# SBUF placement of the FFN weights, tile-by-tile pool waits, and a store that changes its engine, in a one-core transformer block

## The chip, the cores and the metric

The program runs on one core of a Trainium2 chip. The metric is device time in microseconds (us) from one launch, as the median of several runs. A profiled execution gives the trace that is read here. The engines are TensorE (PE in the profile; its weight loads are PEld), VectorE (DVE), ScalarE (ACT), GpSimd (POOL) and SyncE (SP), which only issues DMA transfers.

## The reference

The kernel computes one transformer block in float32: 512 tokens, a width of 2048, and a hidden width of 5632.

```python
mod_x = jnp.split(silu(c) @ w_ada + b_ada, 6, -1)          # and the same for the context
px = modulate(x, sh1, sc1) @ w_in                          # 2048 -> 7168; context: 4096 columns
ox = bidirectional gated linear attention, 8 heads, states from the 256 context tokens
yx = concat([ox, pool mixer, short convolution]) @ w_out   # 2048 -> 2048
x  = layer_norm(ALPHA * x + g1 * yx)
u, g = split(modulate(x, sh2, sc2) @ w_up)                 # 2048 -> 2 x 5632
fx = (u * silu(dwconv3(g) + b)) @ w_down                   # convolution along rows of 64 tokens
return layer_norm(ALPHA * x + g2 * fx)
```

About half of the time goes into the last two products, `w_up` and `w_down`.

## The kernel before

Every large product is made of three float32r matmuls (`mm3`, L109 to L113): both operands are split into a rounded high part and the rest, and hi x hi (L111), hi x lo (L112) and lo x hi (L113) are added in PSUM. In a matmul one operand is stationary (128 x 128, loaded ahead) and the other moves through (256 or 512 columns).

The stages, with the times of the profiled execution:

- 0 to 396 us, ramp: the first modulations and products with `w_in` (tiles `rc`, `rx`, `px_*`).
- To 900 us, attention heads (`lv`, `Q`, `T`, `U`) mixed with further products; then the local mixers.
- About 1000 to 1360 us: `out_half` (`w_out`), `norm_mid` (layer norm, modulation, transposes; writes the activations `h2h`, `h2l`), and `up_half` for the first four of 44 row blocks of `w_up`, which covers the time until all activations exist. `combine` makes the sums S1 to S4 of activations.
- 1375 to 2191 us, up blocks: `up_pair` (L1029) for 20 pairs of row blocks, each with one `up_block` (L997) for the gate half (`ub_g`) and one for the value half (`ub_u`). An up block multiplies 2 x 2 blocks with seven products in place of eight. Its weights are the stationary operand. `weights7` (L976 to L995) loads a tile W (two DMAs, 1 MB together, from SP, L986), combines it on DVE (L989 to L991), and `parts` splits it into H (ACT cast, L972) and L (DVE subtraction, L973). There are 2 buffers of W and 3 each of H and L; one W gives two H and two L. Each up block takes 168 matmuls of 256 columns: 72 with `h2` as the moving operand, 96 with S1 to S4.
- DVE and ACT then put the gate together (L935 to L937, L1038, L1039) and DVE multiplies u with it (L1044); the result h is stored to DRAM (L1045, 256 KB each).
- 2191 to 2644 us, `down` (L1101): h comes back from DRAM (`hr`, L1064) and is split into `hh`, `hl` (or `hb`, both halves in one tile from another pool, for some row blocks). Here h is the stationary operand, and the weights of `w_down` (tiles H_dn, L_dn) move with 512 columns. The work is cut into portions of 15, 14, 12 and 3 row blocks; the last is `finish` (L1122) with the closing layer norm.

Tiles come from pools. Some stacks of pools grow from the left end of SBUF, others from the right. When a pool ends, the next one gets its memory; before that the wait was one for all: the first tile of the new pool waits until every operation on the old pool is done. The scheduler sets the order of each engine's instructions from the program and priorities; `high_priority(offset=AHEAD)` puts the loads and splits of weights ahead of their place. SP's queue runs in order: an issue that waits holds up all behind it.

Addresses: each partition's tiles start at multiples of 32 bytes, and nearly all tiles are multiples of 512 bytes long, so a few small tiles at the start of a stack (`edge_right`, `edge_left`, columns of constants) set the start of everything above, modulo 512. Before, the right side starts at 384 (activations `a2`, S1 to S4, `hh`, `hl`, all weights) and the `h2` and `hb` tiles on the left at 448.

Of the kernel before, what the change touches and what calls it, by code (L numbers as in the profile page):

```python
# [9 lines left out]
F32 = mybir.dt.float32  # L10
# [6 lines left out]
P = 128  # L17
# [26 lines left out]
def vw(ap, dims, off=0):  # L44

    return bass.AP(tensor=ap.tensor, offset=ap.offset + off,
                   ap=[list(ap.ap[0])] + [list(d) for d in dims])
# [25 lines left out]
class Kernel:  # L73
    def __init__(self, ctx, tc, I, out):
        self.tc, self.nc, self.I, self.out = tc, tc.nc, I, out
        self.ctx = ctx
        self.persist = ctx.enter_context(tc.tile_pool(name="persist", bufs=1))
        self.edge = ctx.enter_context(tc.tile_pool(name="edge", bufs=1, side="right"))
        self.edge.tile([P, 24], F32, name="edge_right")
        self.acts = ctx.enter_context(tc.tile_pool(name="acts", bufs=1, side="right"))  # L80
        self.dram = ctx.enter_context(tc.tile_pool(name="spill", bufs=1, space=bass.MemoryType.DRAM))
        self.ps = ctx.enter_context(tc.tile_pool(name="ps", bufs=1, space=PSUM))
        self.ahead = 0
# [51 lines left out]
    def setup(self):  # L135
        nc, I, pp = self.nc, self.I, self.persist
        self.ident = pp.tile([P, P], F32, name="ident")
        make_identity(nc, self.ident)
        self.ones = pp.tile([P, 32], F32, name="ones")
        nc.vector.memset(self.ones, 1.0)  # L140
        self.ones_r = pp.tile([P, P], F32R, name="ones_r")
        nc.scalar.copy(out=self.ones_r, in_=vw(self.ones[:, :], [[0, 4], [1, 32]]))
        self.mhalf = pp.tile([P, 4], F32, name="mhalf")
        nc.vector.memset(self.mhalf, -0.5)
        self.zero = pp.tile([P, 1], F32, name="zero")
        nc.vector.memset(self.zero, 0.0)
        self.cols = {}
        self.persist.tile([P, 8], F32, name="edge_left")

    def columns(self, pool, parts, name):  # L150

# [788 lines left out]
    def up_half(self, cp, p, hf):  # L940

        nc, w = self.nc, self.I["w_up"][0]
        banks = self.banks4(f"up_{p}_{hf}")
        n = 256
        for s in (1, 0):
            for q in (0, 2, 1, 3):
                wh, wl = self.wload(f"up_{p}_{hf}_{s}_{q}",
                                    w[512 * q:512 * q + 512, s * DFF + 256 * p:s * DFF + 256 * p + 256], 4, 256)
                for j in range(4):
                    k = 4 * q + j  # L950
                    h, l = self.h2[hf][k // 2]
                    es = slice((k % 2) * 256, (k % 2) * 256 + 256)
                    for i in range(2):
                        self.mm3(banks[2 * s + i][:, 0:n], (wh[:, j, i * P:(i + 1) * P], wl[:, j, i * P:(i + 1) * P]),
                                 (h[:, es], l[:, es]), start=(k == 0), stop=(k == KT - 1))
        for i in range(2):
            f = 2 * p + i
            u, g = banks[i][:, 0:n], banks[2 + i][:, 0:n]
            c = cp.tile([P, n], F32, name=f"cv_{f}_{hf}", tag="cv", bufs=2)
            s = cp.tile([P, n], F32, name=f"cs_{f}_{hf}", tag="cs", bufs=2)  # L960
            self.gate_conv(f, g, c)
            nc.scalar.activation(out=s, in_=c, func=AF.Sigmoid)
            nc.gpsimd.tensor_tensor(out=s, in0=c, in1=s, op=ALU.mult)
            nc.vector.tensor_tensor(out=c, in0=u, in1=s, op=ALU.mult)
            nc.sync.dma_start(out=self.h_d[f][:, hf * 256:hf * 256 + 256], in_=c)

    def parts(self, ww, name, src, n):

# [60 lines left out]
    def up_pair(self, ww, ep, hx, p):  # L1029
        nc, w = self.nc, self.I["w_up"][0]  # L1030
        g = self.up_block(ww, ep, f"g{p}", w[:, DFF + 256 * p:DFF + 256 * p + 256])
        cs = []
        for i in range(2):
            f = 2 * p + i
            c = hx.tile([P, 512], F32, name=f"cv_{f}", tag="hq", bufs=8)
            s = hx.tile([P, 512], F32, name=f"cs_{f}", tag="hq", bufs=8)
            self.gate_conv(f, g[i], c)
            nc.scalar.activation(out=s, in_=c, func=AF.Sigmoid)  # L1038
            nc.vector.tensor_tensor(out=c, in0=c, in1=s, op=ALU.mult)  # L1039
            cs.append(c)  # L1040
        u = self.up_block(ww, ep, f"u{p}", w[:, 256 * p:256 * p + 256])
        for i in range(2):
            f = 2 * p + i
            nc.vector.tensor_tensor(out=cs[i], in0=u[i], in1=cs[i], op=ALU.mult)  # L1044
            nc.sync.dma_start(out=self.h_d[f], in_=cs[i])  # L1045

    def down_load(self, dn):

# [126 lines left out]
    def run(self):  # L1175
        tc, nc = self.tc, self.nc
        self.setup()
        self.mods2 = self.persist.tile([P, 4 * KT], F32, name="mods2")
        self.o = [None] * KT
        self.h_d = [self.dram.tile([P, L], F32, name=f"h_d{f}") for f in range(NFF)]  # L1180
        self.y_d = [self.dram.tile([P, 4, 512], F32, name=f"y_d{t}") for t in range(NTT)]
        self.g2_d = self.dram.tile([1, D], F32, name="g2_d")
        self.y, self.h2, self.S, self.h = {}, ({}, {}), {}, {}
        self.upc = 0
        with tc.tile_pool(name="wts", bufs=1, side="right") as self.wts:
            with tc.tile_pool(name="xp", bufs=1) as xp:
                self.xp = xp
                with tc.tile_pool(name="rp", bufs=1) as rp:
                    self.setup_columns1(rp)
                    self.load_in(xp, rp)  # L1190
                    self.setup_columns2(rp)
                    T0, V0 = self.ramp(xp, rp)
                with tc.tile_pool(name="gp", bufs=1) as gp:
                    self.bg, self.bg_due, self.tails = self.ada_rest(gp), 0.0, []
                    self.heads(xp, gp, T0, V0)
                    self.local(gp)
                    for _ in self.bg:
                        pass
                    self.split_o()
            hctx = ExitStack()  # L1200
            hx = hctx.enter_context(tc.tile_pool(name="hx", bufs=1))
            with tc.tile_pool(name="cp", bufs=1) as cp:
                st0 = self.out_half(cp, 0)
                self.norm_mid(cp, hx, 0, st0)
                st1 = self.out_half(cp, 1)
                for p in range(SPLIT_PAIRS):
                    self.up_half(cp, p, 0)
                raw = self.norm_mid(cp, hx, 1, st1)
                nc.sync.dma_start(out=self.g2_d.rearrange("o (k p) -> (o p) k", p=P), in_=self.mods2[:, 3 * KT:4 * KT])
                for p in range(SPLIT_PAIRS):  # L1210
                    self.up_half(cp, p, 1)
                    self.combine(cp, raw, (2 * p, 2 * p + 1))
        with tc.tile_pool(name="ww", bufs=1, side="right") as ww:
            with tc.tile_pool(name="ep", bufs=1) as ep:
                for p in range(SPLIT_PAIRS, NFF // 2):
                    self.up_pair(ww, ep, hx, p)
            hctx.close()
            with tc.tile_pool(name="dn", bufs=1) as dn:
                f0 = 0
                for i, n in enumerate(PORTIONS[:-1]):  # L1220
                    self.down(ww, dn, f0, n, i == 0)
                    f0 += n
                self.finish(ww, dn, f0, PORTIONS[-1])
# [28 lines left out]
```

## Time and profile before

| what | value |
|---|---|
| runs | 2696.9, 2699.03, 2702.64 us (median 2699.03) |
| profiled execution | 2703.39 us, its span 2701.6 us, mean granted clock 0.989 |
| PE busy | 2573.6 us, 95% |
| DVE busy | 1895.1 us, 70% |
| ACT, POOL busy | 941.6 us (35%), 225.7 us (8%) |
| HBM read, written | 393.59 MB, 19.93 MB |
| first up block to first down matmul | 1375.0 to 2191.2 us |

How it is read: a window of the trace gives the busy time of each engine in a stretch and, in brackets, the number of instructions. The groups of instructions give the mean duration of one; PE's ends are modelled, and matmuls overlap, so a matmul of 283 ns can start every 119 ns. The chain of waits is followed back from the last instruction and shows at each step what released the next; a wait's row reads total, times, longest. In the names, `ub_g<-h2h,H_g` is: output, moving operand, stationary operand or the reverse.

### The profile page before, as it was taken

What the parts mean: (1) busy time and instruction counts of PE and PEld (TensorE: products, weight loads), DVE (VectorE), ACT (ScalarE), POOL (GpSimd) and SP (SyncE); (2) the same over time, 40 slices, a digit from 0 to 9 for tenths busy, and PEclk for the clock granted to TensorE, in tenths of its full rate; (3) what the DMA queues carried; (4) which work ended last, traced back from release to release, by engine and by line L of the source; (5) the groups of instructions that cost most, each with busy time, mean ns of one, the idle gap of its engine ahead of it and who ended that gap; (6) DMA issues with size and microseconds to landing.
All of it is one profiled execution on the core that took longest, in us unless ns stands there. A gap on an engine that the chain in (4) does not pass through costs nothing.

```text
span 2701.6 us, 40017 instructions
## 1 busy us (share of the span) xinstructions
PE 2573.6 (95%) x16332; PEld 2261.4 (84%) x16332; DVE 1895.1 (70%) x2390; ACT 941.6 (35%) x1127; POOL 225.7 (8%) x207
## 2 busy tenths in 40 slices
PE   5999999999999999989979999999999999999996
PEld 4677978878787787868879999999999988888885
DVE  5534689696968735688888888888888864434338
ACT  4222443232323224444644443443443433222111
POOL 0111022040404000000100000000000000000004
PEclk9999999999999999999989999999999999999998
DMA  8755356646463534666633333333333374333321
GB/s 265 250 194 187 121 198 199 218 136 214 138 221 131 169 97 160 204 213 212 189 104 125 126 103 124 122 106 119 109 122 114 117 245 161 136 121 119 118 94 63
DMA packets 311125, 416.15 MB, mean 154 GB/s; under 512 B 17860, under 2 KB 200476, under 8 KB 310428
## 3 DMA queue, kind: packets, MB, share of 16 engines
q1 hardware_dynamic: 310940, 413.59, 46.6%
q8 instruction: 128, 2.10, 0.3%
q14 instruction: 57, 0.47, 0.0%
HBM read 393.59 MB, written 19.93 MB: 153 GB/s over the span
## 4 chain that ended last, share of the span: by engine, by line
PE 69%; DVE 14%; DMA 8%; issue 5%; ACT 2%; POOL 1%; SPq 1%; DVEq 0%; ACTq 0%; POOLq 0%
PE dn L113 5%; PE dn L112 5%; PE dn L111 5%; PE ub_g L111 3%; PE ub_g L113 3%; PE ub_g L112 3%; DMA W_u<-in_w_up_dram 3%; PE ub_u L111 3%; PE ub_u L113 3%; PE ub_u L112 3%; DMA W_g<-in_w_up_dram 2%; DVE L_g L973 2%; PE wo L112 2%; PE wo L111 2%; PE wo L113 2%
## 5 line engine op out<-in xcount | busy, mean ns | idle before, releaser
L973 DVE TENSOR_TENSOR L_dn<-W_dn,H_dn 128x1536 fp32r<-128x1536 f32 (+1 forms) x56 | 96.2, 1718 | 207.9 <-ACT H_dn L972 207.9
L972 ACT CAST H_u<-W_u 128x1792 fp32r<-128x1792 f32 x80 | 134.1, 1692 | 230.2 <-DVE W_u L991 158.2
L688 DVE SCALAR_TENSOR_TENSOR aacc<-a,csil,aacc 128x512 f32<-128x512 f32 x240 | 180.2, 751 | 12.9 <-DMA a<-in_w_ada_dram 7.5
L973 DVE TENSOR_TENSOR L_u<-W_u,H_u 128x1792 fp32r<-128x1792 f32 x80 | 161.6, 2020 | 38.0 <-ACT H_u L972 38.0
L111 PE MATMUL dn<-H_dn,hh 128*128 128x512 f32 x480 | 186.4, 389 | 1.4 <-ACT hh L1070 1.4
L112 PE MATMUL dn<-L_dn,hh 128*128 128x512 f32 x480 | 187.0, 390 | 0.0
L113 PE MATMUL dn<-H_dn,hl 128*128 128x512 f32 x480 | 186.7, 390 | 0.0
L972 ACT CAST H_g<-W_g 128x1792 fp32r<-128x1792 f32 x80 | 135.2, 1695 | 123.4 <-DVE W_g L991 46.0
L972 ACT CAST H_dn<-W_dn 128x1536 fp32r<-128x1536 f32 (+1 forms) x56 | 81.3, 1451 | 276.2 <-PE dn L113 275.3
L973 DVE TENSOR_TENSOR L_g<-W_g,H_g 128x1792 fp32r<-128x1792 f32 x80 | 161.4, 2018 | 2.4 <-ACT H_g L972 2.4
L111 PE MATMUL ub_g<-h2h,H_g 128*128 128x256 f32 x480 | 135.6, 283 | 14.9 <-ACT H_g L972 14.9
L125 POOL TENSOR_TENSOR ln_r<-ln_e,mhalf 128x1 f32<-128x1 f32 x12 | 9.3, 784 | 1636.0 <-DVE ln_e L120 1405.6
L113 PE MATMUL ub_g<-h2h,L_g 128*128 128x256 f32 x480 | 135.5, 283 | 4.5 <-DVE L_g L973 4.5
L113 PE MATMUL ub_u<-h2h,L_u 128*128 128x256 f32 x480 | 134.3, 280 | 4.4 <-DVE L_u L973 4.4
L112 PE MATMUL ub_g<-h2l,H_g 128*128 128x256 f32 x480 | 134.9, 281 | 0.0
L111 PE MATMUL ub_u<-h2h,H_u 128*128 128x256 f32 x480 | 134.6, 280 | 0.0
L112 PE MATMUL ub_u<-h2l,H_u 128*128 128x256 f32 x480 | 133.9, 279 | 0.0
L106 DVE TENSOR_TENSOR wl_wo<-wr_wo,wh_wo 128x1024 fp32r<-128x1024 f32 x64 | 78.3, 1223 | 49.4 <-ACT wh_wo L105 49.3
L111 PEld LDWEIGHTS dn<-H_dn,hh 128*128 128x128 f32 x480 | 90.1, 188 | 20.6 <-ACT hh L1070 1.8
L113 PEld LDWEIGHTS dn<-H_dn,hl 128*128 128x128 f32 x480 | 90.1, 188 | 19.3 <-DVE hl L1071 0.6
L112 PE MATMUL wo<-wl_wo,oh 128*128 128x512 f32 x256 | 102.7, 401 | 3.7 <-DVE wl_wo L106 3.6
L112 PEld LDWEIGHTS dn<-L_dn,hh 128*128 128x128 f32 x480 | 90.1, 188 | 19.2 <-DVE L_dn L973 0.4
(445 smaller groups left out, 8370.7 us busy)
## 6 DMA issues: line engine op xcount, KB each, us to landing
a<-in_w_ada_dram SPq DMA_DIRECT2D x256, 256.0 KB, 4.3
W_g<-in_w_up_dram SPq DMA_DIRECT2D x80, 512.0 KB, 4.6
W_u<-in_w_up_dram SPq DMA_DIRECT2D x80, 512.0 KB, 4.6
W_dn<-in_w_down_dram SPq DMA_DIRECT2D x24, 1536.0 KB, 6.8
wr_wo<-in_w_out_dram SPq DMA_DIRECT2D x64, 512.0 KB, 4.4
ada<-in_w_ada_dram SPq DMA_DIRECT2D x56, 512.0 KB, 5.0
wr_r<-in_w_in_dram SPq DMA_DIRECT2D x48, 512.0 KB, 3.7
wr_up<-in_w_up_dram SPq DMA_DIRECT2D x32, 512.0 KB, 4.5
```

The lines of the kernel that those rows point to most:

```text
L106: (lo_engine or nc.vector).tensor_tensor(out=lo, in0=raw, in1=hi.bitcast(F32), op=ALU.subtract)
L111: mm(out=out, lhsT=st[0], rhs=mv[0], start=start, stop=False)
L112: mm(out=out, lhsT=st[0], rhs=mv[1], start=False, stop=False)
L113: mm(out=out, lhsT=st[1], rhs=mv[0], start=False, stop=stop)
L125: nc.gpsimd.tensor_tensor(out=r, in0=t, in1=self.mhalf[:, 0:n], op=ALU.pow)
L688: nc.vector.scalar_tensor_tensor(out=acc, in0=raw, scalar=self.csil[:, k:k + 1], in1=acc, op0=ALU.mult, op1=ALU.add)
L972: nc.scalar.copy(out=H[:, 0:n], in_=src)
L973: nc.vector.tensor_tensor(out=Lw[:, 0:n], in0=src, in1=H[:, 0:n].bitcast(F32), op=ALU.subtract)
```

## The change

Three things are done at once.

1. Placement. `edge_right` shrinks from 24 to 16 floats, `edge_left` goes, and a pool `gap` with one tile of 112 floats (448 bytes) is laid on the right side ahead of the pool `ww` (the weights of the up blocks and of the down projection). The activations on both sides now start at 416 modulo 512, the weights in `ww` at 480, the weights of the stages before at 416 or, for the context's first products, at other places.
2. Waits at pool borders. The nine pools outside the persistent ones, and `gap`, get `reuse_waits="tile"`: a new tile waits only for the operations on those old tiles whose memory it takes.
3. The stores of h (L965, L1045; 8 halves and 40 whole tiles) are issued by GpSimd in place of SP.

```diff
-        self.edge.tile([P, 24], F32, name="edge_right")
+        self.edge.tile([P, 16], F32, name="edge_right")
...
-        self.persist.tile([P, 8], F32, name="edge_left")
...
-            nc.sync.dma_start(out=self.h_d[f][:, hf * 256:hf * 256 + 256], in_=c)
+            nc.gpsimd.dma_start(out=self.h_d[f][:, hf * 256:hf * 256 + 256], in_=c)
...
-            nc.sync.dma_start(out=self.h_d[f], in_=cs[i])
+            nc.gpsimd.dma_start(out=self.h_d[f], in_=cs[i])
...
-        with tc.tile_pool(name="wts", bufs=1, side="right") as self.wts:
-            with tc.tile_pool(name="xp", bufs=1) as xp:
+        with tc.tile_pool(name="wts", bufs=1, reuse_waits="tile", side="right") as self.wts:
+            with tc.tile_pool(name="xp", bufs=1, reuse_waits="tile") as xp:
...
+        gap = self.ctx.enter_context(tc.tile_pool(name="gap", bufs=1, side="right", reuse_waits="tile"))
+        gap.tile([P, 112], F32, name="gap_right")
+        with tc.tile_pool(name="ww", bufs=1, reuse_waits="tile", side="right") as ww:
+            with tc.tile_pool(name="ep", bufs=1, reuse_waits="tile") as ep:
...
-            with tc.tile_pool(name="dn", bufs=1) as dn:
+            with tc.tile_pool(name="dn", bufs=1, reuse_waits="tile") as dn:
```

The pools `rp`, `gp`, `hx` and `cp` get the same argument. On PE, DVE and ACT the order of the instructions hardly moves; on SP and POOL the stores do. Line numbers after the change are one lower behind the removed `edge_left`.

SP's queue at the border between `up_half` and the up blocks, before (`wr_up`: weights of up_half, `h_d`: the stored h, `hr`: h for the down projection, `W_g`, `W_u`: weights of the up blocks; in brackets the semaphores that the row waits for):

```order
L100 DMA wr_up_1_0_1_11885<-in_w_up_dram 128x4x256 [waits DMAHW2_49,DVE_49]
L100 DMA wr_up_1_0_3_11915<-in_w_up_dram 128x4x256 [waits DMAHW5_49,DVE_49]
L965 DMA h_d_87<-cv_1_11945 128x256 [waits DVE_49]
L965 DMA h_d_88<-cv_1_11954 128x256 [waits DVE_49]
L1064 DMA hr_20664<-h_d_85 128x512 [waits DMAHW3_49,PE_49]
L986 DMA W_g_0_12023<-in_w_up_dram 128x4x256 [waits DMAHW2_49,DMAHW1_49,DMAHW4_49,DMAHW0_49,DMAHW6_49,DVE_49,DMAHW7_49,PE_49,Pool_49]
L986 DMA W_g_0_12023<-in_w_up_dram 128x4x256
L986 DMA W_g_1_12121<-in_w_up_dram 128x4x256 x2
```

The same place after the change:

```order
L100 DMA wr_up_1_0_1_11884<-in_w_up_dram 128x4x256 [waits DMAHW6_49,DVE_49]
L100 DMA wr_up_1_0_3_11914<-in_w_up_dram 128x4x256 [waits DMAHW7_49,DVE_49]
L1063 DMA hr_20667<-h_d_84 128x512 [waits DMASW4_49,DMASW0_49,PE_49]
L985 DMA W_g_0_12026<-in_w_up_dram 128x4x256 [waits PE_49,Pool_49]
L985 DMA W_g_0_12026<-in_w_up_dram 128x4x256
L985 DMA W_g_1_12124<-in_w_up_dram 128x4x256 [waits DVE_49]
L985 DMA W_g_1_12124<-in_w_up_dram 128x4x256
```

The two stores of h are gone from here, the first W_g waits for PE and POOL alone, and the second one for DVE (the operation S4l, the last of `combine`). On DVE the first operation on W_g stands behind S4l, before and after:

```order
L917 TENSOR_TENSOR S2l_12003<-m_1_7_11382,S2h_12002 128x512 [waits Activation_49]
L917 TENSOR_TENSOR S4l_12007<-a_3_11987,S4h_12006 128x512 [waits Activation_49]
L988 TENSOR_TENSOR W_g_0_12026<-W_g_0_12026 128x4x2x128 [waits DMAHW5_49,DMAHW4_49]
L989 TENSOR_TENSOR W_g_0_12026<-W_g_0_12026 128x4x128 [waits DVE_49]
L990 TENSOR_TENSOR W_g_0_12026<-W_g_0_12026 128x4x128 [waits DVE_49]
```

Only the waits of the row L988 differ from before (it waited for two further transfers and DVE). GpSimd's queue in up_half and the up blocks after the change (`cs`: the gate times its sigmoid, `cv`: the product to be stored):

```order
L962 TENSOR_TENSOR cs_1_11945<-cv_1_11944,cs_1_11945 128x256 [waits Activation_49]
L962 TENSOR_TENSOR cs_1_11954<-cv_1_11953,cs_1_11954 128x256 [waits Activation_49]
L964 DMA h_d_86<-cv_1_11944 128x256 [waits DVE_49]
L964 DMA h_d_87<-cv_1_11953 128x256 [waits DVE_49]
L1044 DMA h_d_88<-cv_12229 128x512 [waits DMASW0_49,DVE_49]
L1044 DMA h_d_89<-cv_12236 128x512 [waits DMASW1_49,DVE_49]
```

The stores follow each other there with nothing between them until the end of the down projection; before, GpSimd had no instruction in the up blocks.

More of the change, by code (lines that the diff above doesn't have):

```diff
@@ L1184, in run @@
         self.upc = 0
-        with tc.tile_pool(name="wts", bufs=1, side="right") as self.wts:
-            with tc.tile_pool(name="xp", bufs=1) as xp:
+        with tc.tile_pool(name="wts", bufs=1, reuse_waits="tile", side="right") as self.wts:
+            with tc.tile_pool(name="xp", bufs=1, reuse_waits="tile") as xp:
                 self.xp = xp
-                with tc.tile_pool(name="rp", bufs=1) as rp:
+                with tc.tile_pool(name="rp", bufs=1, reuse_waits="tile") as rp:
                     self.setup_columns1(rp)
@@ L1192, in run @@
                     T0, V0 = self.ramp(xp, rp)
-                with tc.tile_pool(name="gp", bufs=1) as gp:
+                with tc.tile_pool(name="gp", bufs=1, reuse_waits="tile") as gp:
                     self.bg, self.bg_due, self.tails = self.ada_rest(gp), 0.0, []
@@ L1200, in run @@
             hctx = ExitStack()
-            hx = hctx.enter_context(tc.tile_pool(name="hx", bufs=1))
-            with tc.tile_pool(name="cp", bufs=1) as cp:
+            hx = hctx.enter_context(tc.tile_pool(name="hx", bufs=1, reuse_waits="tile"))
+            with tc.tile_pool(name="cp", bufs=1, reuse_waits="tile") as cp:
                 st0 = self.out_half(cp, 0)
@@ L1212, in run @@
                     self.combine(cp, raw, (2 * p, 2 * p + 1))
-        with tc.tile_pool(name="ww", bufs=1, side="right") as ww:
-            with tc.tile_pool(name="ep", bufs=1) as ep:
+        gap = self.ctx.enter_context(tc.tile_pool(name="gap", bufs=1, side="right", reuse_waits="tile"))
+        gap.tile([P, 112], F32, name="gap_right")
+        with tc.tile_pool(name="ww", bufs=1, reuse_waits="tile", side="right") as ww:
+            with tc.tile_pool(name="ep", bufs=1, reuse_waits="tile") as ep:
                 for p in range(SPLIT_PAIRS, NFF // 2):
```

## The prediction

> **What bounds the kernel now.** I read the page first: the busy shares and the slices.
>
> ```profile
> PE 2573.6 (95%) x16332; PEld 2261.4 (84%) x16332; DVE 1895.1 (70%) x2390; ACT 941.6 (35%) x1127; POOL 225.7 (8%) x207
> PE   5999999999999999989979999999999999999996
> DVE  5534689696968735688888888888888864434338
> ```
>
> TensorE (PE) is nearly always busy, but the average hides two stages with different limits. The windows by stage come next. The first two lie in the up blocks, the third in the down projection.
>
> ```profile
> 1400.00:1700.00 300.00, 300.00 (x2519) 300.00 (x2518) 264.94 (x269) 128.06 (x107) 0.00 (x0) 1.00 0.35 116
> 1700.00:2000.00 300.00, 292.83 (x2443) 291.45 (x2443) 256.70 (x262) 118.48 (x100) 0.00 (x0) 1.00 0.35 115
> 2250.00:2550.00 300.00, 300.00 (x1312) 245.96 (x1311) 117.38 (x124) 66.83 (x59) 0.00 (x0) 1.00 0.37 126
> ```
>
> The columns are PE, weight loads, VectorE (DVE), ScalarE (ACT), GpSimd (POOL), clock, DMA share and GB/s. In the down projection PE is full and nothing else is: a shorter matmul there is a shorter kernel. In the first up window PE is full too, and 300 us over 2519 matmuls are 119.1 ns each, so a pair of blocks (336 matmuls) takes 40.0 us of PE. In the second window PE has gaps. The chain of waits says why; these are the ends of one lap of it:
>
> ```profile
> 1658.40 2.03 DVE L_g L973
> 1660.86 5.57 DMA W_u<-in_w_up_dram
> 1666.53 1.23 DVE W_u L989
> 1671.94 4.56 DMA W_u<-in_w_up_dram
> 1699.04 2.03 DVE L_g L973
> ```
>
> The last subtraction out of a weight buffer (L973) lets the next load into it start, that load lands, DVE combines it, and so on round. From the first to the last row, the same instruction one pair later, are 40.64 us: the feed loop runs a little slower than PE's 40.0 us. The waits in the window 1400 to 2180 agree: PE is kept waiting only by L973, and DVE by the loads.
>
> ```profile
> DVE W_u L989 <- DMA W_u<-in_w_up_dram: 32.3, 38, 2.9
> DVE W_g L989 <- DMA W_g<-in_w_up_dram: 22.5, 23, 2.8
> PE ub_g L113 <- DVE L_g L973: 4.5, 4, 1.7
> PE ub_u L113 <- DVE L_u L973: 4.4, 3, 1.7
> ```
>
> So the up blocks are bound by the feed, with PE close behind. They begin and end at these two starts (chain, then timeline):
>
> ```profile
> 1375.00 0.58 PE ub_g L111
> 2191.18 0.40 PE L111 MATMUL dn<-H_dn,hh 128*128 128x512 f32 x1
> ```
>
> That is 816.2 us for 6720 matmuls, or 121.5 ns of room for each. This is the point from which a slower block matmul costs time; a faster one than 119 brings next to nothing.
>
> **Change, part 1: the pools wait tile by tile.** The one large PE gap that a pool border makes stands ahead of the first up block:
>
> ```profile
> L111 PE MATMUL ub_g<-h2h,H_g 128*128 128x256 f32 x480 | 135.6, 283 | 14.9 <-ACT H_g L972 14.9
> 1363.77 0.61 DVE S4l L918
> 1364.51 0.38 SPq L986
> 1364.95 5.00 DMA W_g<-in_w_up_dram
> 1370.07 1.24 DVE W_g L989
> 1373.26 1.69 ACT H_g L972
> ```
>
> The first weight load is issued only when the last operation of the pools below it (S4l) is done. After the change it waits for an old transpose of norm_mid and for a POOL power; what stands ahead of it in SP's queue is the last load of up_half and a load of h whose stores were out before.
>
> ```profile
> 1337.91 0.81 SPq L965 DMA_DIRECT2D h_d<-cv  x2
> 1339.97 8.59 SPq L100 DMA_DIRECT2D wr_up<-in_w_up_dram  x4
> ```
>
> So it can be issued near 1348.6 and has landed by some 1355. In DVE's order its L989 still follows S4l, so it starts at 1364.4 in place of 1370.07: **5.6 us** earlier. The second weight tile still waits for S4l, and lands 1364.95 + 5.00 = 1369.95 at the latest; DVE needs it only after its three operations on the first. The bounds are 0 (second tile or casts hold it) and 14.9 us (the whole gap). I take 5.6, and since the feed loop begins there, all that follows shifts with it.
>
> At the earlier border (ramp to heads) the chain has a stretch with nothing but issue, and PE waits behind it:
>
> ```profile
> 395.91 1.48 issue
> 397.39 0.68 DVE g L532
> 399.90 1.27 PE lv L573 x7
> PE lv L573 <- DVE Q L589: 4.6, 4, 3.6
> ```
>
> DVE's own work follows it in any case, so of the 3.6 us at most 1.48 can go, and none if another tile's wait ends there: I take **1.0**. At the last border (up to down) PE idles 1.4 us:
>
> ```profile
> L111 PE MATMUL dn<-H_dn,hh 128*128 128x512 f32 x480 | 186.4, 389 | 1.4 <-ACT hh L1070 1.4
> ```
>
> I take **1.0** of it, between 0 and 1.4.
>
> **Part 2: h stored by GpSimd.** Forty stores leave SP's queue in the blocks. SP's wait for them is long but nothing late stands behind it:
>
> ```profile
> SPq L1045 <- DVE cv L1044: 133.5, 38, 7.6
> 1957.86 1.54 SPq L1045 DMA_DIRECT2D h_d<-cv  x2
> 1961.00 0.93 SPq L986 DMA_DIRECT2D W_u<-in_w_up_dram  x2
> DMA to landing us min/median/max: 2.0/2.0/9.1
> ```
>
> The two stores are issued by 1959.40, and the next weight load waits until 1961.00 for its buffer, not for them: gain 0. GpSimd is idle in the blocks (0.00 in the windows), so nothing queues behind the waiting stores there. The stores land 2.0 us after issue, at about 1961.4, just as the weight load starts. If GpSimd's path adds 1 us, they overlap a load of 4.6 us that the loop waits for. Price between 0 and 1 us a pair; I take **0**, as the store is a quarter of the load's size and most of it is out before. The Trainium skill (SBUF — State Buffer, the box on "DVE blocks DMA") speaks against this edit: descriptors of a GpSimd DMA cannot be written while DVE holds the shared port in a two-port mode. DVE does 265 of 300 us here, though in two-operand forms; no run here shows such a store, and by that rule the price is at the upper end, 1 us a pair or above.
>
> **Part 3: placement.** Worked out from pads and tile sizes: in the blocks the stationary weights lay level with the activations S (modulo 512 bytes) and 64 bytes below h2; now 64 above both. In the down projection the weights are the moving operand: the stationary hh, hl lay level with them and hb 64 above; now all lie 64 below. In up_half the 64 below becomes level. What the trace shows of these distances, by form:
>
> ```profile
> L111 PE MATMUL ub_u<-h2h,H_u 128*128 128x256 f32 x478 | 134.0, 280 | 0.0
> L111 PE MATMUL ub_u<-S4h,H_u 128*128 128x256 f32 x160 | 45.4, 284 | 0.0
> L112 PE MATMUL ub_u<-S3l,H_u 128*128 128x256 f32 x160 | 45.3, 283 | 0.0
> L112 PE MATMUL dn<-L_dn,hh 128*128 128x512 f32 x467 | 181.9, 390 | 0.0
> L112 PE MATMUL dn<-L_dn,hb 128*128 128x512 f32 x176 | 69.6, 396 | 0.0
> L111 PE MATMUL rc<-hch,wh_r 128*128 128x256 f32 x240 | 68.5, 285 | 0.0
> L113 PE MATMUL up<-h2h,wl_up 128*128 128x256 f32 x256 | 72.9, 285 | 5.1 <-DVE wl_up L106 5.0
> ```
>
> With the stationary 64 below, a matmul takes 280 against 283.5 level, 3 less; with it 64 above (hb), 396 against 390, 6 more; 128 apart (rc) is like level. Two distances that the change brings in are not shown: 64 above at 256 columns, 64 below at 512.
>
> *Down projection*: 1440 matmuls go from level to 64 below, 528 from 64 above to 64 below. At the price of 256 columns that is 1440 x 3 ns = 4.3 and 528 x (6 + 3) ns = 4.8, together **9.1 us** off. The 144 of the last portion would give 1.3 more, but the chain there runs on DVE, so 0. If instead distance counts without sign, 1440 get 6 ns longer: 8.6 us on. I take the sign as shown and keep both.
>
> *Up blocks*: if the role counts as in hb, 6 ns more on level: 120 + 6 = 126 ns, over the room of 121.5. If it stays in the band of the other distances (280 to 285), the feed hides it. I take **0**: at 256 columns the row that I can see for "apart" is below or at level, and hb differs from hh in its pool and tile shape too. But this is the weakest step.
>
> *up_half*: 768 matmuls 3 ns longer are 2.3 us; DVE makes PE wait 5.0 us there, so part hides: **+1.5**. The projections rc move from 128 to other distances: +-3, taken as 0.
>
> On placement the Trainium skill (TensorE: Matmul & The Clock Gate, Part 2, loading the weights) says that PE reads stationary and moving operand through two independent ports, so that loading one takes nothing from the other. By that the whole of part 3 would be 0; hb against hh, 396 to 390 ns, disagrees.
>
> **Sum** against the profiled execution's 2703.4: -5.6 - 1.0 - 1.0 + 0 - 9.1 + 0 + 1.5 = -15.2 us. That execution lies 4.4 us above the median of the runs, 2699.0, so the median becomes **2684**.
>
> **The rivals.**
>
> *B, block matmuls slow down (slower).* The 64 above at 256 columns costs as in hb: 126.3 ns, 6720 x 126.3 = 848.7 us. PE then sets the blocks' end. Its first 5 us run at half the granted clock, 21 matmuls in place of 42, which is 2.5 us more:
>
> ```profile
> 1375.00:1380.00 5.00, 5.00 (x21) 4.72 (x22) 4.96 (x4) 1.53 (x1) 0.00 (x0) 0.50 0.00 0
> ```
>
> It starts at 1375.0 - 5.6 = 1369.4 and ends at 2220.6, 29.4 later than 2191.2. With -9.1, -2.0 and +1.5 that is +20: **2719**. For it: the only row with this distance. Against it: other columns, other pool. It decides from 121.5 ns on.
>
> *C, placement has no effect* (the two ports of the skill's rule). Left are -5.6 - 1.0 - 1.0: **2691**. Against it stand 280 beside 284 and 390 beside 396.
>
> *D, GpSimd's stores collide with the loads.* The chain lies on the feed loop from about 1650 to 2191, 13 pairs: 13 x 1 us on the forecast, **2697**. Against it: the stores have landed when the load starts, so that only what GpSimd's path adds can overlap.
>
> *E, 512 columns dislike 64 in either direction*: +8.6 in place of -9.1: **2702**. For it: 64 above does cost; against it: h2.
>
> **How the numbers follow.** Forecast 0.40, B 0.24, C 0.14, D 0.10, E 0.12. What the runs can tell from no change is 0.2%, 5.4 us. Faster by more: forecast, C and a little of D, 0.56. Within: most of D and half of E, 0.16. Slower: B and the rest of E, 0.28. The forecast's own range is 2676 to 2691 (first load 0 to 14.9, the down term to 6). To hold eight in ten it must reach up almost to B, and down for a larger gap or down term: 2666 to 2717.
>
> **What would show it.** First step: the idle time ahead of the first ub_g falls from 14.9 to about 9, and the W_g load is issued ahead of S4l. Down term: the dn groups read 386 to 387, with no group at 396. Blocks: the time from the first ub_g to the first dn stays within 2 us of 816; PE waits for L973 remain. If these waits vanish while the windows of the blocks show fewer than 2460 matmuls in 300 us, B holds. If L989 waits longer for its loads than 55 us in all, D holds. What would make the forecast wrong above all is a block matmul over 121.5 ns.

## The result and the profile after

The changed kernel takes 2713.8 us (median of 6, 2710.5 to 2720.7) against 2700.6 us for the kernel before, measured again beside it: a ratio of 1.0052, 95% interval 1.0037 to 1.0067. It is half a per cent **slower**; the forecast was 0.6% faster.

The page of the changed kernel first. PE is busy for nearly as long as before (2560.7 us against 2573.6), DVE too; a software queue for GpSimd's stores is new. The chain of waits is of no use here ("issue 51%"): it loses its thread. That is not the stores' doing, as the kernels e1 and e4 below, with all stores on SP, read 52% and 51%.

```profile
span 2715.1 us, 40075 instructions
PE 2560.7 (94%) x16332; PEld 2239.3 (82%) x16332; DVE 1893.2 (70%) x2390; ACT 938.2 (35%) x1127; POOL 251.9 (9%) x255
q0 software_dynamic: 3584, 11.54, 1.1%
issue 51%; PE 36%; DVE 6%; POOL 3%; ACT 2%; DMA 2%; SPq 0%; POOLq 0%; DVEq 0%; ACTq 0%
L111 PE MATMUL ub_g<-h2h,H_g 128*128 128x256 f32 x480 | 134.3, 280 | 8.8 <-ACT H_g L971 8.8
L111 PE MATMUL ub_u<-h2h,H_u 128*128 128x256 f32 x480 | 132.9, 277 | 0.0
```

The up blocks have moved at both ends (timeline of PE, first block matmul and first matmul of the down projection):

```profile
1361.33 0.58 PE L111 MATMUL ub_g<-h2h,H_g 128*128 128x256 f32 x1 [8.77 <-ACT H_g L971]
2206.04 0.39 PE L111 MATMUL dn<-H_dn,hh 128*128 128x512 f32 x1
```

They begin 13.7 us earlier (1375.0 before) and end 14.9 us later (2191.2): 844.7 us in place of 816.2. From there to the end are 509.1 us, 510.4 before. So the whole loss, and more, lies in the blocks. The windows by stage say what PE does there:

```profile
1365.00:1700.00 335.00, 315.96 (x2674) 312.08 (x2675) 278.62 (x281) 131.79 (x111) 7.63 (x14) 0.98 0.34 111
1700.00:2000.00 300.00, 280.19 (x2364) 276.06 (x2363) 250.17 (x254) 117.04 (x100) 7.64 (x14) 0.98 0.35 112
2250.00:2550.00 300.00, 300.00 (x1312) 246.14 (x1312) 121.12 (x130) 71.94 (x68) 0.00 (x0) 1.00 0.39 130
```

In 300 us only 2364 matmuls, where there were 2443, and 20 us idle where there were 7. Yet a single matmul is *faster*: 277 ns (h2) in place of 280. From the starts of consecutive matmuls in the records, where PE does not wait, one starts every 113.9 ns; before it was 120 level and 117.8 with the weights 64 below. So PE waits. The waits (window 1400 to 2120; before, the same four rows read 30.1, 19.1, 4.4 and 2.7) say for what: PE waits for DVE's subtraction L, and DVE in turn for the loads.

```profile
DVE W_u L988 <- DMA W_u<-in_w_up_dram: 50.1, 34, 3.6
DVE W_g L988 <- DMA W_g<-in_w_up_dram: 25.3, 24, 3.0
PE ub_u L113 <- DVE L_u L972: 21.9, 25, 2.4
PE ub_g L113 <- DVE L_g L972: 19.7, 16, 3.3
```

The feed loop (load, combination on DVE, subtraction, release of the buffer, next load) has become longer: from one pair's last subtraction L_u to the next pair's are 42.3 us in the mean, in place of 40.9. PE, faster than before, stands still for it.

### The profile page after: what moved, and what is told of

Read it like the earlier page. It is cut to its first block, busy times and chain, and to the rows that moved or that the text cites. A ratio compares the mean times of both kernels' runs of the same rounds, so it can differ in the third digit from the quotient of the medians.

```text
span 2715.1 us, 40075 instructions
## 1 busy us (share of the span) xinstructions
PE 2560.7 (94%) x16332; PEld 2239.3 (82%) x16332; DVE 1893.2 (70%) x2390; ACT 938.2 (35%) x1127; POOL 251.9 (9%) x255
## 4 chain that ended last, share of the span: by engine, by line
issue 51%; PE 36%; DVE 6%; POOL 3%; ACT 2%; DMA 2%; SPq 0%; POOLq 0%; DVEq 0%; ACTq 0%
PE px_f L111 2%; PE px_f L112 2%; PE px_f L113 2%; PE wo L112 2%; PE wo L113 2%; PE wo L111 2%; PE rc L113 1%; PE rc L111 1%; PE ada L280 1%; PE rc L112 1%; PE px_g L111 1%; PE px_g L113 1%; PE px_g L112 1%; PE px_v L111 1%; PE px_v L113 1%
## 5 line engine op out<-in xcount | busy, mean ns | idle before, releaser
L113 PEld LDWEIGHTS ub_g<-h2h,L_g 128*128 128x128 f32 x480 | 91.6, 191 | 30.8 <-DVE L_g L972 30.5
L113 PEld LDWEIGHTS ub_u<-h2h,L_u 128*128 128x128 f32 x480 | 90.3, 188 | 28.9 <-DVE L_u L972 28.8
```

The costliest lines, as they stand in the source:

```text
L113: mm(out=out, lhsT=st[1], rhs=mv[0], start=False, stop=stop)
```

## The experiments

Every ratio is against the kernel before, measured again beside the run. "Blocks" is the time from the first ub_g to the first dn, "start" the first ub_g; both are of the one profiled execution of each kernel, which can lie some us from the median of its runs (e3: 2713.1 against 2708.2 us; e10: 2689.7 against 2682.4). W start is where the weight tiles of the blocks begin, modulo 512; before it is 384.

| run | what it is | ratio, 95% interval | start | blocks |
|---|---|---|---|---|
| before | | 1 | 1375.0 | 816.2 |
| changed | all three parts, W start 480 | 1.0052 [1.0037, 1.0067] | 1361.3 | 844.7 |
| e1 | changed, all stores on SP | 1.0010 [0.9998, 1.0022] | 1369.4 | 825.4 |
| e2 | before, stores on GpSimd | 1.0037 [1.0023, 1.0051] | 1371.5 | 820.6 |
| e3 | before, new placement | 1.0013 [0.9997, 1.0029] | 1370.6 | 827.4 |
| e4 | before, tile-by-tile waits | 0.9993 [0.9984, 1.0001] | 1369.9 | 819.7 |
| e5 | changed, block stores on SP | 0.9994 [0.9980, 1.0009] | 1363.3 | 826.9 |
| e6 | e3, but W start 0 | 0.9976 [0.9966, 0.9986] | 1375.0 | 807.2 |
| e7 | before, everything at 416 | 0.9985 [0.9973, 0.9998] | 1370.6 | 818.2 |
| e9 | e5 with halved weight tiles | 0.9776 [0.9760, 0.9793] | 1358.0 | 768.2 |
| e10 | e5, but W start 0 | 0.9935 [0.9913, 0.9956] | 1361.6 | 809.1 |
| e11 | e9, block stores on GpSimd | 0.9788 [0.9768, 0.9809] | 1360.5 | 768.3 |
| e12 | e9, old placement | 0.9930 [0.9912, 0.9948] | 1364.3 | 807.5 |
| e13 | before, S moved to 64 below W, W start 384 | 1.0019 [1.0007, 1.0032] | 1371.8 | 815.3 |

### One part at a time: e1 to e4

After the result there were two theories for the longer loop: the stores from GpSimd (S), or the placement (P).

e1, the changed kernel with SP's stores again:

```diff
-            nc.gpsimd.dma_start(out=self.h_d[f][:, hf * 256:hf * 256 + 256], in_=c)
+            nc.sync.dma_start(out=self.h_d[f][:, hf * 256:hf * 256 + 256], in_=c)
...
-            nc.gpsimd.dma_start(out=self.h_d[f], in_=cs[i])
+            nc.sync.dma_start(out=self.h_d[f], in_=cs[i])
```

> The changed kernel with the stores of h back on SP; placement and tile-by-tile waits stay. Theory S (the stores from GpSimd are what slows the feed loop of the up blocks): the time from the first ub_g to the first dn falls from 844.7 us to 816 or below, the two stores of a pair land within 3.5 us of each other's start again, and the whole is 2683 to 2690 us. Theory P (the placement slows the feed, since the faster matmuls disturb loads or DVE, or since PE's gaps lower its clock): the blocks stay at 840 to 845 us, the whole at 2710 to 2715.

e2, the reverse edit on the kernel before:

> The kernel before with only the stores of h moved to GpSimd. Theory S: the blocks grow from 816.2 us by 15 to 28 (fewer where PE sets the pace in the first pairs), the whole is 2712 to 2728 us. Theory P: no change beyond 0.2%, 2696 to 2706 us.

e3, the kernel before with the pads and the gap pool of the change, without `reuse_waits`, stores on SP:

> The kernel before with only the new placement (pads and the gap pool). Block matmuls start every 114 ns in place of 119. Theory S: the feed at 40.9 us a pair still binds, so the blocks take 812 to 818 us, and the whole is 2695 to 2700 us. Theory P: the blocks take 835 to 845 us, the whole 2718 to 2728 us.

e4, the kernel before with `reuse_waits="tile"` on its nine pools:

> The kernel before with only the tile-by-tile waits of the pools. Both theories: the first ub_g starts earlier and the blocks stay at 816 us. If the waits alone bring the 13.7 us by which the first ub_g of the changed kernel was earlier: 2686 to 2690 us. If half of it came from placement (the products with w_in) or from the stores: 2692 to 2696 us.

Neither theory fits alone, and most of the ranges were missed: e1 and e3 lie between the two theories, the blocks of e2 grew by only 4.4 us in its trace, and e4 gained nothing. Shown is that the stores alone cost 0.37% (2711.2 against 2700.4 us, +10.8). The placement alone brings nothing that can be told, although a block matmul starts some 5 ns sooner after the last: 1.0013 with an interval that holds 1, and single runs that scatter from 2693 to 2714 us. Its profiled execution, a slow one of these, has blocks 11 us longer.

How the stores do it is seen in GpSimd's and SP's timeline of the changed kernel, at one pair:

```profile
1929.37 0.54 POOL L1044 DMA_DIRECT2D h_d<-cv  x1 [41.85 <-DVE cv L1043]
1931.97 0.55 POOL L1044 DMA_DIRECT2D h_d<-cv  x1 [2.06 <-issue]
1932.13 0.93 SPq L985 DMA_DIRECT2D W_u<-in_w_up_dram  x2
1938.06 1.22 DVE L988 TENSOR_TENSOR W_u<-W_u 128x1024 f32<-128x1024 f32 x1 [1.46 <-DMA W_u<-in_w_up_dram]
```

In the kernel before, SP issued the two stores 1.2 us apart, as DVE finished the two products, and each had landed 2.0 us later: the second one within 0.1 us of the issue of the next weight load, whose first packet follows 1.0 us after its issue. GpSimd needs 2.6 us from one to the next, though the second product is done by then, and the stores land later. So the second one (1931.97) goes out together with the load (1932.13), and that load is long. The landings of the stores, first before, then after:

```profile
DMA to landing us min/median/max: 2.0/2.0/2.0
DMA to landing us min/median/max: 2.3/3.4/7.1
```

By the packet records (1024 packets of 1 KB are one weight tile), the load behind the stores takes 5.4 us from its issue to its last packet where no instruction fetch falls into it, the three others of a pair 4.6. Only this one of the four positions is longer in e2 as well (5.3 us). That is 0.7 to 0.8 us a pair, or 14 to 16 us over 20 pairs. Whether DVE's work held GpSimd's stores back, as the prediction considered, no run tells apart.

The waits alone do almost nothing: in e4 the first block starts at 1369.9, barely earlier than in e2 and e3 (1371.5 and 1370.6), which have the old waits. SP's timeline of e4 says why:

```profile
1357.27 0.81 SPq L965 DMA_DIRECT2D h_d<-cv  x2
1358.18 0.39 SPq L1064 DMA_DIRECT2D hr<-h_d  x1
1358.68 2.85 SPq L986 DMA_DIRECT2D W_g<-in_w_up_dram  x4
```

The first W_g could go, but two stores of h stand ahead of it on SP and wait for DVE. Only with those stores elsewhere *and* the waits by tile is the tile in time. The PE gap ahead of the first block is 14.9 us before, 13.7 in e4, 13.1 in e1, and 8.8 in the changed kernel.

### Block stores or half stores: e5

The 40 block stores go back to SP, the 8 of up_half stay on GpSimd.

```diff
-            nc.gpsimd.dma_start(out=self.h_d[f], in_=cs[i])
+            nc.sync.dma_start(out=self.h_d[f], in_=cs[i])
```

> The changed kernel with the 40 stores of the up blocks back on SP, the 8 of up_half left on GpSimd. Theory S (in the blocks the store from GpSimd lands later and delays the fourth weight load of a pair by 0.6 us): the first ub_g stays at 1361 us, the blocks fall from 844.7 to 825 us as with all stores back, the whole is 2693 to 2700 us. Rival (the stores in up_half do the harm, or the early first load does): blocks stay near 840, 2710 or more.

As expected, if a little above the range (2702.2 us): the early start stays (1363.3), the blocks fall to 826.9. From 1.0052 to 0.9994, the block stores cost the changed kernel 0.58%, some 16 us. What is left of the change gains nothing over the kernel before: the blocks start 11.7 us earlier, but they end only 0.9 us earlier (2190.3 against 2191.2).

### Why do faster matmuls lengthen the blocks? e6, e7, e13

Two guesses: the starts at 416 and 480, which are no multiples of 64, slow the loads (M), or the faster PE itself disturbs the loop (F). e6 keeps the distances of e3 and moves all starts, to 448 and 0:

```diff
-        self.edge.tile([P, 16], F32, name="edge_right")
+        self.edge.tile([P, 8], F32, name="edge_right")
...
+        self.persist.tile([P, 8], F32, name="edge_left")
```

> Placement alone as in the run with only the placement, with the same distances (weights 64 above in the blocks, 64 below in the down projection), but all starts at multiples of 64 (448 and 0 in place of 416 and 480). Theory M (starts that are 32 off a multiple of 64 slow the loads): blocks 812 to 818 us, whole 2693 to 2699. Theory F (with faster matmuls the feed is bare from the first pair on, and PE's instruction fetches that fall into a load lengthen the loop): blocks 823 to 830 us, as with the odd starts, whole 2702 to 2712.

e7 puts everything at 416 and level (`edge_right` 16, no `edge_left`, no gap):

> Placement alone, with everything on both sides at 416, so odd starts as in the changed kernel but all weights level with all activations. Block matmuls start every 120 ns. Theory M: blocks 823 to 830 us. Theory F: 814 to 820 us, as before; the down projection loses the 528 matmuls at 233 ns and is 3 us shorter: whole 2694 to 2700.

e6 takes 2696.0 us and its blocks 807.2, 20 us below e3 with the same distances; F is out for that part, as PE is nearly as fast there (a matmul every 115.4 ns in the mean, where PE does not wait, against 114.2). But e7, with odd starts, is not slow, as M had it: its blocks take 818.2 us, and DVE waits for loads 51.2 us against 49.2 in the kernel before (window 1400 to 2120):

```profile
DVE W_u L988 <- DMA W_u<-in_w_up_dram: 32.6, 34, 3.0
DVE W_g L988 <- DMA W_g<-in_w_up_dram: 18.6, 20, 2.6
```

So a start at 0 might be what helps, and not just one at a multiple of 64. e13 separates these: W starts at 384 (a multiple of 64), S at 320, h2 at 448 (`edge_right` 40, `edge_left` 8).

> Placement alone: the weights at 384 as before, S at 320 (weights 64 above), h2 at 448 (weights 64 below), so PE at some 115.5 ns, faster than the feed. Theory A with 512 (only a start at a multiple of 512 loads faster): blocks 813 to 822 us. Theory A with 64 (an odd start is what slows): blocks 805 to 811 us. Accident of phases: 820 to 830.

815.3 us: that is the range for "only a start at a multiple of 512". The packet records agree in one part. From the last packet of a weight tile to DVE's start on it are 0.42 us in the mean where W starts at 0 (e6 and e10 below), and 0.54 to 0.62 in the traces with 384, 416 and 480, wherever DVE waits for the load. The load itself, from issue to last packet, takes 5.00 us in e3, 4.90 in e7, 4.87 in e6, 4.86 in e13 and 4.88 in the kernel before. That does not show that odd starts slow a load: e3 has 14 loads with an instruction fetch in them (next paragraphs), the four others 10 or 11, and without those the medians are 4.59, 4.60, 4.53, 4.57 and 4.57 us. The three traces with W at 480 and all stores of the blocks on SP (e1, e3, e5) do have the longest blocks, 825 to 827 us, but whether the start, the faster PE or the place of the fetches does it is open.

In the waits for loads (window 1400 to 2120), e3, then e13, then e6:

```profile
DVE W_u L988 <- DMA W_u<-in_w_up_dram: 36.4, 34, 3.4
DVE W_g L988 <- DMA W_g<-in_w_up_dram: 26.1, 23, 2.9
```

```profile
DVE W_u L989 <- DMA W_u<-in_w_up_dram: 32.6, 35, 3.3
DVE W_g L989 <- DMA W_g<-in_w_up_dram: 18.9, 21, 2.2
```

```profile
DVE W_u L989 <- DMA W_u<-in_w_up_dram: 27.1, 34, 2.8
DVE W_g L989 <- DMA W_g<-in_w_up_dram: 17.0, 20, 2.7
```

These are 62.5, 51.5 and 44.1 us, in the order of the blocks' times. The whole time of e13 is above that of e6 also because its down projection takes 3 us longer.

A second lengthener is in all these kernels. The chain of waits of e3 has loads of 7 us among those of 4.6; beside them, the DMA queues in the window of each:

```profile
1485.45 7.09 DMA W_g<-in_w_up_dram
1497.68 4.63 DMA W_u<-in_w_up_dram
...
q1 hardware_dynamic: 1056, 1.05, 45.8%
q8 instruction: 1, 0.02, 0.8%
...
q1 hardware_dynamic: 1056, 1.05, 65.9%
```

In the long one there is a packet of instructions (16 KB, one every 15 to 16 us; in e9 below, with a faster PE, one every 14.5 against 15.3 in e12, so they seem to be PE's), in the short one none. Over all loads of e3, 14 with such a packet from the issue to 4 us after it take 6.5 us in the mean, the others 4.7; in the kernel before 10 take 6.2, the others 4.7. Summed over these loads, the excess is 27 us in e3 and 17 in the kernel before, and the difference is nearly the 11 us between their blocks. This is a coincidence in the records, repeated in every kernel, not an experiment: no run took the fetches away. It would fit that the runs of e3 scatter so much, since it is a matter of phases whether a fetch falls into a load that the loop waits for.

### The change without what it lost: e10

e5 with the starts of e6.

> The changed kernel with the block stores on SP and starts at 448 and 0 in place of 416 and 480, distances as changed. Theory A (what the change lost is the store collision and the starts of the weight tiles; the rest of it gains): first ub_g near 1363 us, blocks 805 to 812 us, whole 2682 to 2690. If the better time of the aligned placement was an accident of phases: blocks 820 to 830 us, whole 2698 to 2706, as with the odd starts.

2682.4 us, at the edge of the expectation; blocks 809.1. The early start and the good placement are worth 0.65% together, once the block stores are on SP and the tiles start at 0. It also repeats e6's reading in another kernel, so that it was not an accident. All starts moved together, though: that it is W's start is likely, by the 0.42 us above, but not shown by itself.

The trace of e10 holds something else. PE is full in the first 300 us, yet it starts a matmul only every 117.6 ns, with the weights 64 above as in the changed kernel; and its down projection has 397 ns in all groups, where e6, with the same starts, has 388 to 394 (below, window 1400 to 1700, and one group of the window 2220 to 2690):

```profile
1400.00:1700.00 300.00, 300.00 (x2550) 300.00 (x2549) 265.24 (x270) 126.11 (x104) 0.00 (x0) 1.00 0.36 119
L111 PE MATMUL dn<-H_dn,hh 128*128 128x512 f32 x409 | 162.5, 397 | 0.0
```

From about 1800 us on the blocks of e10 run at 113.4 ns for a while, and e6, mostly nearer to 114, runs at 117.8 from about 1620 to 1800. So at one and the same distance there are two paces, and PE can pass from one to the other within an execution. What makes it change is not shown.

### Taking the feed off the path: e9, e11, e12

If the loop is the limit, shortening it must show what the placement is worth. In e9 the weight tile of the blocks is halved: four tiles of 512 KB in place of two of 1 MB. A tile is then free after one cast and one subtraction, not two, and its load has the time of three others. The down projection gets a pool of its own over the same memory.

```diff
-NB, NU = 4, 2
+NB, NU = 2, 2
...
-            W = ww.tile([P, NB, 7, P], F32, name=f"W_{name}", tag="W", bufs=2)
+            W = self.wu.tile([P, NB, 7, P], F32, name=f"W_{name}", tag="W", bufs=4)
...
-            W = ww.tile([P, 7, 512], F32, name=f"W_{name}", tag="W", bufs=2)
+            W = self.wd.tile([P, 7, 512], F32, name=f"W_{name}", tag="W", bufs=2)
...
+            with tc.tile_pool(name="wu", bufs=1, reuse_waits="tile", side="right") as self.wu:
...
+            with tc.tile_pool(name="wd", bufs=1, reuse_waits="tile", side="right") as self.wd, \
```

> The changed kernel with the block stores on SP and the weight tile W of the up blocks halved: four tiles of 512 KB in place of two of 1 MB, same memory, so a tile is released after one cast and one subtraction in place of two, and the next load starts earlier. Theory F: the wait for the release and the load is what makes the loop; with more loads ahead PE's 113.8 ns a matmul can show: blocks 775 to 800 us, whole 2650 to 2675. Rival (DVE at 88% or DMA itself is the limit): blocks over 812 us, whole 2690 or more.

It takes 2641.1 us, below the expected range: 2.24% faster than the kernel before, and the best of all. The windows and the waits (1400 to 2120) of e9:

```profile
1400.00:1700.00 300.00, 300.00 (x2649) 300.00 (x2648) 282.90 (x379) 132.18 (x110) 0.00 (x0) 1.00 0.40 126
1700.00:2000.00 300.00, 300.00 (x2649) 300.00 (x2648) 282.92 (x379) 132.51 (x111) 0.00 (x0) 1.00 0.40 125
...
DVE W_g L988 <- DMA W_g<-in_w_up_dram: 3.2, 5, 0.9
DVE W_u L988 <- DMA W_u<-in_w_up_dram: 2.5, 4, 1.0
ACT H_u L971 <- PE ub_g L112: 136.6, 53, 3.1
```

PE never idles, 2649 matmuls in 300 us are 113.3 ns each, and the waits have turned round: ACT waits for PE. DVE is at 94%, so it would be the next.

e11 is e9 with the block stores on GpSimd (the edit of e5 undone), e12 is e9 with the pads of the kernel before and no gap.

> The kernel with halved weight tiles, with the block stores on GpSimd again as in the change. Theory F (the stores cost only through the feed loop, which no longer binds): within 0.2% of the 2641 us with the stores on SP. Rival (the stores cost PE or DVE directly, 0.4 to 0.6 us a pair): 2649 to 2655.

> The kernel with halved weight tiles, with the placement of before (level with S, 64 below h2; no gap). Theory F: PE binds in the blocks now, so 119.1 ns in place of 113.3 for 6720 matmuls are 39 us more; blocks 802 to 812 us, whole 2674 to 2684. Rival (DVE or the loads bind, PE's pace does not matter): 2641 to 2650.

e11: 2644.0 us, blocks 768.3 as in e9. The same stores that cost 16 us above cost nothing that can be told here (they land after 2.5 us in the median): their harm goes through the feed loop. e12: 2682.5 us, blocks 807.5, and its window:

```profile
1400.00:1700.00 300.00, 300.00 (x2519) 300.00 (x2519) 271.21 (x364) 127.31 (x106) 0.00 (x0) 1.00 0.38 119
```

2519 against 2649 matmuls: with PE as the limit, the placement is worth 39 us (807.5 - 768.2). In the kernel as it was, it could not show.

## Why the prediction was wrong, by its steps

The range, 2666 to 2717, holds the measured 2713.8, but that is luck: its upper end was there for B, which did not come. The direction was wrong.

- **What bounds the kernel** was right: the up blocks are bound by the feed loop, with PE close behind. What I did not draw from it: on such a loop every tenth of a microsecond on a load that it waits for counts, up to 80 times, while a faster PE counts for nothing.
- **First load, -5.6**: right as a size for both edits together (the gap fell by 6.1 us, the first ub_g came 9 to 10 us earlier than in e2, e3 and e7), wrong as the gain of the waits alone. The step read the new queue, in which the stores of h had left SP, and booked the gain on the waits; e4 shows that with the stores in place it is almost nothing. Wrong too is that "all that follows shifts with it": in e5 the blocks start 11.7 us earlier and end 0.9 us earlier.
- **Block stores, 0 (rival D: up to 1 us a pair)**: this step failed. The trace showed that the stores land just as the weight load starts, and I gave the case 0.10. Measured: 0.7 to 0.8 us on the fourth load of each pair, and +0.37% alone, +0.58% (16 us) in the changed kernel. D's price per pair was about right, but it counted 13 pairs: with the faster PE the loop binds from the first pair on (315.96 of 335 us busy in the first window). Its sign came too, with DVE's waits for loads at 75.4 us, over the 55 named; e3, without such stores, also passes it, with 62.5. I had looked only at when the store would land, not at how far apart GpSimd issues two of them (2.6 us against 1.2). The Trainium skill (DMA: Bandwidth & Descriptors, Specifications, the row on first-byte latency) gives about 1 us for a DMA from GpSimd against 0.6 from SP; the landings here, 2.3 to 3.7 us against 2.0, agree with later, and the distance between two issues is not in that figure.
- **Up blocks, 0**: right that a faster matmul would bring nothing there, but the placement can have another effect that I had not thought of: where the tiles start changes how soon a load can be used. With W at 0 in place of 480 the blocks are 20 us shorter (e6 against e3), and the ratios are 0.9976 and 1.0013. Against the start at 384 of the kernel before, the change lost nothing that can be told (e3).
- **Down term, -9.1**: failed as well, in size. 64 below at 512 columns is not a gain. The groups of the changed kernel read 388, 392 and 394 ns by line:

```profile
L111 PE MATMUL dn<-H_dn,hh 128*128 128x512 f32 x460 | 178.1, 388 | 0.0
L112 PE MATMUL dn<-L_dn,hh 128*128 128x512 f32 x460 | 180.4, 392 | 0.0
L113 PE MATMUL dn<-H_dn,hl 128*128 128x512 f32 x460 | 180.7, 394 | 0.0
```

  They start every 226.0, 229.2 and 231.6 ns, against 226.9 level and 233.4 at 64 above. So 1440 matmuls lost 2 ns and 528 won 4.5: about 0 in all, as the 509.1 against 510.4 us to the end say. Both new distances came out against their neighbours: 64 above, slow at 512 columns, is the fastest at 256; 64 below, fast at 256, is middling at 512, and in e10 it is as slow as 64 above. The short waits at the two other borders did shrink, from 3.6 to 1.7 and from 1.4 us to nothing, as the two terms of 1.0 had it.
- **Rival B (block matmuls slow down)** had the right sign and almost the right time (2719) by the wrong mechanism: block matmuls became faster, and PE's waits for L grew from 7 to 42 us rather than vanishing.
- **Rival C (two independent read ports, so no effect)**: e9 against e12 settles it for this kernel. Both placements have the same reads in the same order with PE the only limit, and 113.3 ns stand against 119.1. By the Trainium skill (TensorE: Matmul & The Clock Gate, Part 2) a weight load takes nothing from the running matmul. The measurement says that the pace of matmuls with their weight loads depends on where the operands start; which of the two reads waits, it does not show.

The way from the forecast to the result, from the runs: the block stores cost 16 us where 0 was booked, the stage from the first dn to the end gained 1.3 us in place of 9.1, and what the early start had gained was lost again in the blocks (e5, level with the kernel before). From e5 to e10 another 0.59% is in the starts of the tiles, which the kernel before had not got either.

What stays open: why a tile that starts at 0 is ready 0.1 to 0.2 us sooner, why the blocks with W at 480 are the longest, why one distance has two paces, and whether the instruction fetches cause the long loads or only go with them.

## What to carry to other kernels

Before making an engine faster, ask whether it is the one that waits; in a feed loop of few buffers it was the loads' latencies, the issue distance of the stores beside them and the starts of the tiles that counted here, and finer tiles in the same memory were worth far more (2.2%) than all three parts of the change. A part that looks useless can be worth 39 us once the limit is elsewhere, so test parts again after the limit has moved. And two edits that only work together (the stores off SP, the waits by tile) show nothing when each is tried alone.

## What the runs showed of the hardware

- The start interval of a matmul changes with the distance, modulo 512 bytes, of its stationary from its moving operand. At 256 columns it was 113.3 ns at +64 (e9, PE never idle), 117.8 at -64 and 120 level; at 512 columns 226.8 level (e7: all groups at 389 ns), 226 to 232 at -64, and 233 at +64.
- The distance does not settle it alone: e10 ran at 117.6 ns with +64 for 300 us and then faster, and at 233 ns with -64 through its down projection.
- Two stores issued by GpSimd followed each other after 2.6 us at the closest (0.54 busy and 2.06 idle), in the kernel before by SP after 0.9 to 1.2, where DVE's products set the distance.
- A 1 MB load into tiles that start at 0 modulo 512 was in DVE's hands 0.42 us after its last packet in the mean, at 384, 416 or 480 after 0.54 to 0.62.
- Loads with an instruction packet (queue q8) in their first 4 us took 6.2 to 6.6 us in the mean of a kernel, others 4.6 to 4.9.
